# Work of GpSimd given to the vector engine, and identity products put between the tensor engine's products, in a four-layer network written by a build-time planner

## The chip, the cores and the metric

One core of a Trainium2 chip runs the whole network in one launch. The metric is the device time of that launch in microseconds (us), the median of several runs. The kernel before has a median of 1254.95 us in three runs (1254.81 to 1259.41).

## The reference

The input is a sequence of 256 rows of 1024 numbers, all fp32. It goes through two blocks of two layers each.

```python
def first_block(x, ...):
    for i in range(2):
        mix = even_mixer(rms_norm(x, norm_mix[i]), ...) if i == 0 else odd_mixer(...)
        x = x + mix
        x = x + sqrelu_mlp(rms_norm(x, norm_mlp[i]), mlp_w1[i], mlp_w2[i])
    return rms_norm(x, norm_final)

def second_block(x, ...):
    for layer in range(2):
        cols = split_columns(rms_norm_2(x, norm_g[layer]) @ w_in[layer])
        y_gdn, y_mla, y_rwkv = gdn_branch(cols, ...), mla_branch(cols, ...), rwkv7_branch(cols, ...)
        mix = concatenate([y_gdn, y_mla, y_rwkv], -1) * silu(cols['gate'])
        x = x + mix @ w_out[layer]
    return rms_norm_2(x, final_norm_g)
```

The even layer holds two kinds of attention with projected q, k, v (one of them over compressed keys too), the odd layer plain causal attention. The gated delta branch (gdn) and the rwkv branch are linear recurrences, evaluated in four chunks of 64 steps: inside a chunk a triangular system is inverted, and a state is carried from chunk to chunk, forward and backward in time. The mla branch is a softmax attention with rotary embeddings.

## The kernel before

The code names tiles and operations in program order. It does not say in which order an engine runs them. `Order.note` (line 265) records every operation with a cost that `Order.cost` (line 282) works out from its sizes, and `Order.plan` (line 396) then places them one by one: for each engine it takes, among the first operations whose inputs are ready, the one that can start earliest, and gives each new tile a place in SBUF or a bank in PSUM. It keeps its own clock for each engine, doubles the cost of a product where its own account of recent tensor work is low, and lengthens a vector operation that overlaps a GpSimd operation by its own account. `flush` (line 373) tries 24 ways of packing the memory, keeps the plan that it believes shortest, and issues all operations through `put` (line 560), so that nearly every row of the profile has the line L561. Semaphores are added from the tiles that operations share. Each engine runs its operations strictly in the planned order.

Within a layer, `weave` (line 1002) steps through parts named in a string ORDER (for instance `gdn_inv*2 rwkv_proj`), which gives the order of recording and with it the priority.

Weights come by `wload` (line 639): a transfer of 512 KB issued by SyncE into the tile wt, a copy on ScalarE that rounds it to fp32r (the tile fr), and a subtraction on VectorE for the rest; a product of full precision is three fp32r products (`mm3`, line 658). Products in plain fp32 appear in the trace with two records each. The q projection of the even layer (`Even.q`, line 1132) loads each half of its 256 columns in four transfers of 128 KB, with runs of 64 columns (256 bytes), in the order that its heads need.

The steps that the change and the prediction touch are these:

- `gdn_uw` (line 1843): the tiles kd[d] = kn * fd, 128x768, on GpSimd (line 1867), next to kg[d] on the vector engine.
- `gdn_steps` (line 1896): the state of the chunk before is scaled by ge into Sn, 128x384, on GpSimd (line 1935), and for one chunk an addition to qs (line 1945).
- `rwkv_prep` (line 2057): half of AR, a product of rT and ec, four times 128x256, on GpSimd (line 2111).
- `rwkv_bonus` (line 2186): an addition of 128x512 (line 2194), and for each half a scale and a product of 128x256 on GpSimd (lines 2198 and 2199). The bonus products of TensorE wait for them.
- `mla_proj` (line 2346): t1 + t2 of the rotary part, 128x256 and 64x256, on GpSimd (line 2444).
- `invert` (line 1586): the triangular inverse by substitution, 30 steps of one product and one addition each on the vector engine, every one needing the step before.
- `comp` (line 1326): 16 small products of 64x128 by 64x16, first the eight of the first half of the partitions, then the eight of the other.

What GpSimd does besides (the masks of `gdn_prep`, the gates of `rwkv_end` and `gdn_end`, some memsets, powers and weight transfers) is not touched.

Of the kernel before, what the change touches and what calls it, by code (L numbers as in the profile page):

```python
# [21 lines left out]
F = mybir.dt.float32  # L22
# [155 lines left out]
class Order:  # L178
# [4 lines left out]
    def __init__(self, nc, sb, wt, fr, ps):  # L183
# [17 lines left out]
        self.phase = 0.0  # L201
        self.ahead = 4000
# [62 lines left out]
    def note(self, eng, method, a, k):  # L265
# [4 lines left out]
        for key, v in k.items():  # L270
            if isinstance(v, bass.AP):
# [8 lines left out]
                         eng == "vector" and sum(self.space(x) == "sb" for x in ins if self.size(x) > 1) > 1))  # L280

    def cost(self, eng, method, outs, ins, k, ps):
# [90 lines left out]
    def flush(self):  # L373
# [16 lines left out]
        for i in self.log:  # L390
            eng, method, a, k = self.ops[i][:4]
            self.put(i, getattr(getattr(self.real, eng), method), [self.place(x) for x in a],
                     {q: self.place(x) for q, x in k.items()})
        self.ops = []

    def plan(self, preds, long, window=600, look=10):
# [35 lines left out]
        held = [0.0, 0.0]  # L432
# [10 lines left out]
        free, last_free = [0.0] * 16, 0.0  # L443

# [21 lines left out]
        while p < n:  # L466
            best = None
            for e in self.ENGINES:
                c, seen = None, 0
                for pr, i in avail[e]:  # L470
                    if i > p + window or seen >= look:
                        break
# [27 lines left out]
            avail[e].remove((pr, i))  # L500
            order.append(i)
# [11 lines left out]
            if method == "dma_start":  # L513
                dma = max(dma, s + cost + 650) + lat
                fin = dma + 900
            elif e == "tensor":
# [9 lines left out]
                gate[win] = gate.get(win, 0) + ops[i][10]  # L526
                fin = s + lat
            else:
                if e == "gpsimd":
                    held = [s, s + cost]  # L530
                elif e == "vector" and ops[i][12]:
                    slow = 0.5 * max(0.0, min(s + cost, held[1]) - max(s, held[0]))
                    cost, lat = cost + slow, lat + slow
                    if slow and now["gpsimd"] == held[1]:
                        held[1] += slow
                        now["gpsimd"] = held[1]
# [27 lines left out]
class Net:  # L564
# [74 lines left out]
    def wload(self, src, r0, nk, c0, nc_, pieces=None):  # L639
# [3 lines left out]
        for h in range(m):  # L643
# [8 lines left out]
            self.nc.scalar.copy(x[:, 0:n], raw)  # L652
            self.sub(x[:, n:2 * n], raw, x[:, 0:n].bitcast(F))
# [92 lines left out]
    def setup(self):  # L746
# [3 lines left out]
        nc.sync.dma_start(self.ident, I["consts"][:, 0:128])  # L750
        self.x = self.t(2048).rearrange("p (t d) -> p t d", t=2)
# [236 lines left out]
class Layer:  # L988

    tag = ""  # L990

    def __init__(self, net):
# [9 lines left out]
    def weave(self, order):  # L1002

        parts, ended = {}, set()
        for word in order.split():
            n, _, steps = word.partition("*")
            if n not in parts:
                m = n.rstrip("0123456789")
# [61 lines left out]
class Even(Layer):  # L1070

    tag = "E"
    ORDER = (
# [252 lines left out]
    def comp(self):  # L1326
# [4 lines left out]
        for g in range(2):  # L1331
            p = self.ps()
            sv = p[:, 0:128].rearrange("p (t j c) -> p t j c", t=2, j=4)
            sl = slice(g * 64, g * 64 + 64)
            for t in range(2):
                for j in range(4):
                    self.mm(sv[:, t, j, :], qT[sl, j, t * 128:(t + 1) * 128], self.ck[sl, :])
# [31 lines left out]
class Odd(Layer):  # L1369

    tag = "O"
    ORDER = (
# [63 lines left out]
class Second(Layer):  # L1436
# [4 lines left out]
    tag = "S"  # L1441

# [400 lines left out]
    def gdn_uw(self):  # L1843
# [52 lines left out]
    def gdn_steps(self):  # L1896
# [7 lines left out]
        for s in range(4):  # L1904
# [20 lines left out]
            if s < 3:  # L1925
# [8 lines left out]
                if s:  # L1934
                    self.mul(Sn, St, self.ge[:, s, :, :, None].to_broadcast([128, 2, 3, 64]), nc.gpsimd)
# [4 lines left out]
            if s:  # L1940
# [3 lines left out]
                if s == 2:  # L1944
                    self.add(qs[:, 1], qs[:, 1], dst, nc.gpsimd)
# [111 lines left out]
    def rwkv_prep(self):  # L2057
# [40 lines left out]
        for d in range(2):  # L2098
# [87 lines left out]
    def rwkv_bonus(self):  # L2186
# [7 lines left out]
        self.add(bo, av[0], av[1], nc.gpsimd)  # L2194
# [347 lines left out]
```

## Time and profile before

| what | value |
|---|---|
| median of three runs | 1254.95 us |
| the profiled execution | 1256.8 us |
| its span, first to last instruction | 1255.0 us |
| outside the span | 1.8 us |
| mean granted clock of TensorE | 0.902 of full speed |
| busy: TensorE, VectorE, ScalarE, GpSimd | 1073.0, 838.6, 576.5, 114.3 us |

In the profile PE is TensorE (PEld its weight loads), DVE is VectorE, ACT is ScalarE, POOL is GpSimd, SP is SyncE. The page's second part cuts the span in 40 slices of 31.4 us, one digit each. The granted clock has two levels, 1.2 and 2.4 GHz; 0.5 and 1.0 in a row are these two, and a number between them a stretch with both. The chain is the sequence of work that ended last, followed backward from the last instruction. A row of tensor work counts records, and busy time of the tensor engine is modelled, so that it may be stalled inside a busy stretch.

### The profile page before, as it was taken

What the parts mean: (1) busy time and instruction counts of PE and PEld (TensorE: products, weight loads), DVE (VectorE), ACT (ScalarE), POOL (GpSimd) and SP (SyncE); (2) the same over time, 40 slices, a digit from 0 to 9 for tenths busy, and PEclk for the clock granted to TensorE, in tenths of its full rate; (3) what the DMA queues carried; (4) which work ended last, traced back from release to release, by engine and by line L of the source; (5) the groups of instructions that cost most, each with busy time, mean ns of one, the idle gap of its engine ahead of it and who ended that gap; (6) DMA issues with size and microseconds to landing.
All of it is one profiled execution on the core that took longest, in us unless ns stands there. A gap on an engine that the chain in (4) does not pass through costs nothing.

```text
span 1255.0 us, 22363 instructions
## 1 busy us (share of the span) xinstructions
PE 1073.0 (85%) x8969; PEld 951.1 (76%) x8969; DVE 838.6 (67%) x1721; ACT 576.5 (46%) x1065; POOL 114.3 (9%) x182
## 2 busy tenths in 40 slices
PE   8998899999998999999997843488998894648895
PEld 7887699999897989999977743478668884647564
DVE  5556765555646585555579897863888899676646
ACT  4565454444427465444454532224574464222742
POOL 0000000000000000000013111002300312311100
PEclk9999899999998999999997965688999896777788
DMA  9930466555635335755743211122223342004100
GB/s 232 286 114 19 137 198 201 183 182 179 196 102 168 125 109 195 243 190 177 247 121 101 78 27 29 56 51 95 85 69 95 105 131 51 19 7 140 51 1 34
DMA packets 133905, 151.51 MB, mean 121 GB/s; under 512 B 24298, under 2 KB 115561, under 8 KB 133801
## 3 DMA queue, kind: packets, MB, share of 16 engines
q1 hardware_dynamic: 132969, 147.89, 37.9%
q0 software_dynamic: 832, 2.20, 0.6%
q8 instruction: 70, 1.15, 0.4%
q14 instruction: 34, 0.28, 0.1%
HBM read 147.42 MB, written 1.07 MB: 118 GB/s over the span
## 4 chain that ended last, share of the span: by engine, by line
PE 58%; DVE 25%; ACT 6%; issue 5%; DMA 4%; POOL 1%; SPq 1%; DVEq 0%; POOLq 0%; ACTq 0%
PE ps L561 58%; DVE sb L561 20%; DVE fr L561 5%; ACT sb L561 5%; DMA wt<-in_ev_w_in 2%; POOL sb L561 1%; ACT fr L561 1%; DMA wt<-in_mlp_w 1%; SPq L561 1%; DMA sb<-in_positions 1%; DMA wt<-in_w_in 0%; DMA sb<-in_norm_mlp 0%; ACT L561 0%; DMA brd<-sb 0%; DVEq L2538 0%
## 5 line engine op out<-in xcount | busy, mean ns | idle before, releaser
L561 PE MATMUL ps<-fr 128*128 128x256 f32 (+3 forms) x5112 | 791.5, 315 | 40.0 <-DVE sb L561 16.7
L561 PEld LDWEIGHTS ps<-fr 128*128 128x128 f32 (+1 forms) x5112 | 715.7, 194 | 100.2 <-DVE fr L561 17.2
L561 PE MATMUL ps<-sb 64*64 64x64 f32 (+12 forms) x3857 | 307.6, 285 | 131.1 <-DVE sb L561 97.2
L561 PEld LDWEIGHTS ps<-sb 64*64 64x64 f32 (+4 forms) x3857 | 240.5, 170 | 192.4 <-DVE sb L561 91.0
L561 DVE TENSOR_TENSOR fr<-wt,fr 128x1024 fp32r<-128x1024 f32 (+2 forms) x265 | 315.9, 1222 | 52.8 <-ACT fr L561 51.9
L561 ACT CAST fr<-wt 128x1024 fp32r<-128x1024 f32 (+2 forms) x265 | 262.5, 1034 | 71.0 <-DMA wt<-in_mlp_w 22.4
L561 ACT ACTIVATE sb<-sb 128x256 f32<-128x256 f32 (+7 forms) x347 | 163.3, 502 | 221.4 <-DVE sb L561 200.3
L561 DVE TENSOR_TENSOR sb<-ps,sb 128x256 f32<-128x256 f32 (+7 forms) x169 | 86.5, 518 | 170.9 <-ACT sb L561 91.7
L561 ACT ACTIVATE sb<-ps 128x384 f32<-128x384 f32 (+7 forms) x166 | 77.6, 475 | 247.3 <-PE ps L561 211.0
L561 DVE TENSOR_TENSOR sb<-sb 128x24 f32<-128x24 f32 (+27 forms) x408 | 142.4, 357 | 17.9 <-POOL sb L561 4.8
L561 DVE SCALAR_TENSOR_TENSOR sb<-sb 128x256 f32<-128x256 f32 (+8 forms) x228 | 94.8, 434 | 35.4 <-ACT sb L561 30.2
L561 POOL TENSOR_TENSOR sb<-sb 128x384 f32<-128x384 f32 (+4 forms) x83 | 88.0, 1080 | 294.8 <-DVE sb L561 184.1
L561 DVE TENSOR_TENSOR sb<-sb,ps 128x512 f32<-128x512 f32 (+3 forms) x82 | 46.8, 582 | 29.2 <-PE ps L561 28.9
L561 ACT ACTIVATE sb<-ps,sb 128x256 f32<-128x256 f32 (+3 forms) x70 | 35.0, 541 | 55.0 <-PE ps L561 48.2
L561 POOL TENSOR_SCALAR sb<-sb 128x2 f32<-128x2 f32 (+2 forms) x12 | 6.2, 515 | 415.3 <-DVE sb L561 304.4
L561 DVE TENSOR_TENSOR fr<-sb,fr 128x512 fp32r<-128x512 f32 (+1 forms) x38 | 24.7, 649 | 21.5 <-ACT fr L561 21.3
L561 POOL MEMSET sb<- 128x2 f32 (+3 forms) x59 | 5.6, 138 | 351.4 <-DVE sb L561 286.4
L561 ACT CAST fr<-sb 128x512 fp32r<-128x512 f32 x32 | 19.9, 622 | 31.5 <-DVE sb L561 31.5
L561 DVE COPY sb<-ps 128x384 f32<-128x384 f32 (+9 forms) x45 | 21.4, 478 | 17.0 <-PE ps L561 15.7
L561 DVE TENSOR_SCALAR sb<-sb 128x2 f32<-128x2 f32 (+15 forms) x115 | 27.2, 252 | 4.7 <-POOL sb L561 2.0
L561 DVE CUSTOM_DVE_ANT_0 sb<-ps,sb 128x128 f32<-128x128 f32 (+1 forms) x80 | 24.7, 353 | 6.7 <-PE ps L561 3.5
L561 ACT ACTIVATE fr<-ps,sb 128x256 fp32r<-128x256 f32 x52 | 19.8, 486 | 11.3 <-PE ps L561 10.6
(30 smaller groups left out, 162.7 us busy)
## 6 DMA issues: line engine op xcount, KB each, us to landing
wt<-in_mlp_w SPq DMA_DIRECT2D x128, 512.0 KB
wt<-in_w_in SPq DMA_DIRECT2D x38, 512.0 KB
wt<-in_od_w_in SPq DMA_DIRECT2D x24, 512.0 KB
wt<-in_w_out SPq DMA_DIRECT2D x16, 512.0 KB
wt<-in_ev_w_in SPq DMA_DIRECT2D x14, 512.0 KB
wt<-in_ev_w_out SPq DMA_DIRECT2D x8, 512.0 KB
wt<-in_od_w_out SPq DMA_DIRECT2D x8, 512.0 KB
wt<-in_w_in SPq DMA_DIRECT2D x8, 384.0 KB
```

The source lines that it names most:

```text
L561: fn(*a, **k)
```

## The change

There are six parts.

1. Five kinds of operation go from GpSimd to VectorE: kd in `gdn_uw`, Sn and the addition to qs in `gdn_steps`, half of AR in `rwkv_prep`, the addition, scales and products of `rwkv_bonus`, and t1 + t2 in `mla_proj`.

```diff
-            self.mul(f12(self.kd[d]), f12(kn), b(self.fd), self.nc.gpsimd)
+            self.mul(f12(self.kd[d]), f12(kn), b(self.fd))
...
-                    self.mul(Sn, St, self.ge[:, s, :, :, None].to_broadcast([128, 2, 3, 64]), nc.gpsimd)
+                    self.mul(Sn, St, self.ge[:, s, :, :, None].to_broadcast([128, 2, 3, 64]))
...
-                    self.add(qs[:, 1], qs[:, 1], dst, nc.gpsimd)
+                    self.add(qs[:, 1], qs[:, 1], dst)
...
-                self.mul(od(AR[h][:, :, 1, d], d), c4(rT[:, h]), ec[d][:, h, :, 1 - d:65 - d], nc.gpsimd)
+                self.mul(od(AR[h][:, :, 1, d], d), c4(rT[:, h]), ec[d][:, h, :, 1 - d:65 - d])
...
-        self.add(bo, av[0], av[1], nc.gpsimd)
+        self.add(bo, av[0], av[1])
...
-            self.ts(bo[:, h], bo[:, h], ka[:, h:h + 1], ka[:, 2 + h:3 + h], eng=nc.gpsimd)
-            self.mul(bo[:, h], bo[:, h], kT[:, h], nc.gpsimd)
+            self.ts(bo[:, h], bo[:, h], ka[:, h:h + 1], ka[:, 2 + h:3 + h])
+            self.mul(bo[:, h], bo[:, h], kT[:, h])
...
-            self.add(t1[:m], t1[:m], t2[:m], nc.gpsimd)
+            self.add(t1[:m], t1[:m], t2[:m])
```

2. The planner places products of the identity with itself. When it is about to place a tensor operation that it expects to start at s, it first fills the time up to s: as long as a product fits with 100 ns to spare, a PSUM bank is free, and its account of recent tensor work is under a limit, it issues one fp32 product of 128x128 by 128x128 into the bank that has been free longest. Nobody reads the result.

```diff
+            if e == "tensor" and hot and done[hot[0]] and uses[hot[1]]:
+                t, got = max(last_free, warm_from), self.arenas["ps"].find(1)
...
+                while got:
+                    t = max(t + self.switch(cut, (128, 128)), got[0])
...
+                    if t + took + self.spare > s or sum(x[1] for x in past) > self.dense * self.warm:
+                        break
+                    order.append(-1 - got[1][0])
...
+                    free, last_free, now[e] = [t] * 16, t, t
...
         for i in self.log:
+            if i < 0:
+                ar, x = self.arenas["ps"], self.place(self.idle)
+                self.real.tensor.matmul(ar.tile[:, (-1 - i) * ar.unit:(-1 - i) * ar.unit + 128], x, x, start=True, stop=True)
+                continue
```

3. The planner's costs change: a GpSimd operation is taken as shorter, and an overlap of the two engines lengthens both by factors that depend on the kind of vector operation.

```diff
-        c = 100 + n * per.get(method, 1.0) + (165 * n if k.get("op") == OP.pow else 0)
+        c = 60 + n * 0.8 * per.get(method, 1.0) + (165 * n if k.get("op") == OP.pow else 0)
...
+    def share(self, method, outs, ins):
+        if any(self.space(x) == "ps" for x in outs + ins):
+            return 0.0, 0.25
+        if method in ("tensor_copy", "tensor_scalar", "memset"):
+            return 0.75, 0.2
+        return (0.47, 0.5) if sum(self.size(x) > 1 for x in ins) > 1 else (0.0, 0.4)
```

4. The q weights of the even layer come in two transfers per half with runs of 128 columns (512 bytes). The reordering by heads moves into two copies and two subtractions of 128x512 with a stride in place of one each of 128x1024.

```diff
-        w = self.load(0, pieces=[(i * 64, (2 * c + i // 2 + 4 * (i % 2)) * 64, 64) for i in range(4)])
+        w = self.load(0, pieces=[(g * 128, (2 * c + 4 * g) * 64, 128) for g in range(2)], heads=True)
...
+                for j in range(2):
+                    self.nc.scalar.copy(xv[:, 0, :, j], rj[:, :, :, j])
+                    self.sub(xv[:, 1, :, j], rj[:, :, :, j], xv[:, 0, :, j].bitcast(F))
```

5. In `comp` the 16 small products alternate between the two halves of the partitions, into two banks.

```diff
+        for t in range(2):
+            for j in range(4):
+                for g in range(2):
+                    sl = slice(g * 64, g * 64 + 64)
+                    self.mm(svs[g][:, t, j, :], qT[sl, j, t * 128:(t + 1) * 128], self.ck[sl, :])
```

6. Assertions on the order of the parts are added, and a separate look-ahead for SyncE with the same value, 600, as the others had. The ORDER strings are the same.

## Rows read from the trace of the kernel before

**Rows 1.** The page's clock in 40 slices, chain by engine; span and clock by core.
```profile
PEclk9999899999998999999997965688999896777788
...
PE 58%; DVE 25%; ACT 6%; issue 5%; DMA 4%; POOL 1%; SPq 1%; DVEq 0%; POOLq 0%; ACTq 0%
...
core 0: 1255.0 us, clock 0.902
```

**Rows 2.** Busy time by stretch: length, PE, PEld, DVE, ACT, POOL, clock, DMA.
```profile
718.00:854.00 136.00, 76.04 (x1072) 68.91 (x1071) 102.41 (x229) 35.42 (x58) 11.75 (x12) 0.65 0.18 49
...
1038.00:1142.00 104.00, 57.62 (x986) 53.26 (x986) 76.63 (x172) 23.68 (x39) 26.81 (x26) 0.69 0.16 41
1158.00:1201.00 43.00, 36.96 (x294) 26.02 (x294) 23.38 (x66) 30.12 (x66) 6.61 (x9) 0.68 0.10 38
```

**Rows 3.** The chain's shares in the three stretches of rows 2, in order.
```profile
by line: DVE sb L561 46.4%; PE ps L561 33.3%; ACT sb L561 7.8%; issue 6.2%; DVE fr L561 4.7%; ACT fr L561 1.3%; DVEq L561 0.2%; ACTq L561 0.2%
...
by line: DVE sb L561 50.3%; PE ps L561 25.4%; POOL sb L561 9.6%; issue 7.6%; DVE fr L561 5.6%; ACT sb L561 2.2%; DVEq L561 0.1%; POOLq L561 0.1%
...
by line: PE ps L561 51.1%; DVE sb L561 27.8%; ACT sb L561 8.5%; issue 7.5%; DVE fr L561 5.8%; ACT fr L561 2.2%; DVEq L561 0.1%; ACTq L561 0.0%
```

**Rows 4.** Who TensorE waited for, whole span: total us, times, longest.
```profile
PE ps L561 <- DVE sb L561: 113.9, 52, 13.9
PE ps L561 <- ACT sb L561: 25.5, 26, 3.5
```

**Rows 5.** Columns of rows 2: two stretches of fp32r products, two of 64x64 products.
```profile
738.00:742.00 4.00, 4.00 (x21) 4.00 (x20) 3.91 (x11) 0.00 (x0) 0.00 (x0) 0.50 0.67 175
...
958.00:962.00 4.00, 4.00 (x36) 4.00 (x35) 4.00 (x11) 0.93 (x2) 0.00 (x0) 1.00 0.77 241
...
1090.00:1094.00 4.00, 4.00 (x108) 4.00 (x102) 1.18 (x2) 0.81 (x1) 0.00 (x0) 0.55 0.01 4
1094.00:1098.00 4.00, 2.60 (x99) 2.19 (x94) 2.57 (x3) 3.04 (x5) 0.52 (x1) 1.00 0.02 4
```

**Rows 6.** TensorE in order of time: start, length, form, records; the wait before.
```profile
946.35 1.93 PE L561 MATMUL ps<-sb 128*128 128x128 f32 x16
...
122.32 2.65 PE L561 MATMUL ps<-sb 64*128 64x16 f32 x24 [1.13 <-DVE sb L561]
```

**Rows 7.** GpSimd by form: busy us, mean ns of one, idle before.
```profile
L561 POOL TENSOR_TENSOR sb<-sb 128x256 f32<-128x256 f32 x26 | 25.7, 1004 | 143.8 <-DVE sb L561 71.5 <-ACT sb L561 59.2 <-PE ps L561 12.8
L561 POOL TENSOR_TENSOR sb<-sb 128x768 f32<-128x768 f32 x4 | 8.3, 2091 | 18.4 <-DVE sb L561 18.4
```

**Rows 8.** VectorE by form: busy us, mean ns of one, idle before.
```profile
L561 DVE TENSOR_TENSOR sb<-sb 128x256 f32<-128x256 f32 x34 | 15.2, 480 | 6.0 <-ACT sb L561 4.7 <-PE ps L561 1.0
...
L561 DVE TENSOR_SCALAR sb<-sb 128x256 f32<-128x256 f32 x22 | 7.6, 377 | 1.4 <-ACT sb L561 1.3
...
L561 DVE TENSOR_TENSOR sb<-sb 128x768 f32<-128x768 f32 x6 | 6.0, 1016 | 1.2 <-POOL sb L561 1.2
```

**Rows 9.** The chain near 1080 us, GpSimd's pieces, first and last: start, length.
```profile
1075.96 4.80 POOL sb L561 x2
...
1083.84 1.31 POOL sb L561
```

**Rows 10.** VectorE in order of time, with and without a 768-wide GpSimd operation beside.
```profile
728.51 1.42 DVE L561 TENSOR_TENSOR sb<-sb 128x58 f32<-128x58 f32 x1
...
730.18 0.20 DVE L561 TENSOR_TENSOR sb<-sb 128x58 f32<-128x58 f32 x1
```

**Rows 11.** DMA from 4 to 8 us, then from 48 to 52 us: packets, bytes, engines' share.
```profile
DMA packets 3132, 1.05 MB, mean 264 GB/s; under 512 B 2985, under 2 KB 3018, under 8 KB 3132
...
q1 hardware_dynamic: 3132, 1.05, 117.1%
...
DMA packets 1458, 1.46 MB, mean 364 GB/s; under 512 B 42, under 2 KB 1457, under 8 KB 1457
...
q1 hardware_dynamic: 1457, 1.45, 107.0%
```

More of the change, by code (lines that the diff above doesn't have):

```diff
@@ L201, in __init__ @@
         self.phase = 0.0
+        self.idle = None
+        self.dense, self.spare = 2.2, 100
+        self.reach = 600
         self.ahead = 4000
@@ L279, in note @@
                          self.mode(outs, ins) if eng == "tensor" else None,
-                         eng == "vector" and sum(self.space(x) == "sb" for x in ins if self.size(x) > 1) > 1))
+                         self.share(method, outs, ins) if eng == "vector" else None))
     def cost(self, eng, method, outs, ins, k, ps):
@@ L443, in plan @@
         free, last_free = [0.0] * 16, 0.0
+        hot, warm_from, past = None, 0.0, []
+        if self.idle is not None:
+            t = self.split(self.idle)[0]
+            hot = first[t], t
         def start(i, e):
@@ L469, in plan @@
                 c, seen = None, 0
+                far = p + (self.reach if e == "sync" else window)
                 for pr, i in avail[e]:
-                    if i > p + window or seen >= look:
+                    if i > far or seen >= look:
                         break
@@ L500, in plan @@
             avail[e].remove((pr, i))
+            if e == "tensor" and hot and done[hot[0]] and uses[hot[1]]:
+                t, got = max(last_free, warm_from), self.arenas["ps"].find(1)
+                past = [x for x in past if x[0] > t - 3413]
+                while got:
+                    t = max(t + self.switch(cut, (128, 128)), got[0])
+                    win = int((t + self.phase) / 3413.3)
+                    took = 420 if gate.get(win - 1, 0) < self.warm else 223
+                    if t + took + self.spare > s or sum(x[1] for x in past) > self.dense * self.warm:
+                        break
+                    order.append(-1 - got[1][0])
+                    cut = (128, 128)
+                    gate[win] = gate.get(win, 0) + 512
+                    past.append((t, 512))
+                    t += took
+                    free, last_free, now[e] = [t] * 16, t, t
+                    self.arenas["ps"].since[got[1][0]] = t + 200
+                    self.arenas["ps"].cache = {}
+                if cut is not None and ops[i][11][0] != cut:
+                    s = max(s, last_free + self.switch(cut, ops[i][11][0]))
             order.append(i)
@@ L515, in plan @@
                 fin = dma + 900
+                if hot and i == hot[0]:
+                    warm_from = fin
             elif e == "tensor":
@@ L529, in plan @@
                 if e == "gpsimd":
[L530 to L536, printed above, removed]
+                    more = sum(f * max(0.0, min(s + cost, y) - max(s, x)) for x, y, f in recent)
+                    cost, lat = cost + more, lat + more
+                    held = [s, s + cost, i]
+                elif e == "vector":
+                    f, g = ops[i][12]
+                    both = max(0.0, min(s + cost, held[1]) - max(s, held[0]))
+                    if both:
+                        cost, lat = cost + f * both, lat + f * both
+                        if now["gpsimd"] == held[1]:
+                            held[1] += g * both
+                            now["gpsimd"] = held[1]
+                            for j in succ[held[2]]:
+                                ready[j] = max(ready[j], held[1] + 50)
+                    recent.append((s, s + cost, g))
+                    del recent[:-8]
                 fin = s + lat
@@ L750, in setup @@
         nc.sync.dma_start(self.ident, I["consts"][:, 0:128])
+        self.order.idle = self.ident
         self.x = self.t(2048).rearrange("p (t d) -> p t d", t=2)
@@ L990 @@
     tag = ""
+    NEEDS = {}
     def __init__(self, net):
@@ L1007, in weave @@
             if n not in parts:
+                assert ended >= set(self.NEEDS.get(n, "").split()), (n, ended)
                 m = n.rstrip("0123456789")
@@ L1330, in comp @@
         nc.vector.memset(lc, BIG)
[L1331 to L1337, printed above, removed]
+        svs = [self.ps()[:, 0:128].rearrange("p (t j c) -> p t j c", t=2, j=4) for _ in range(2)]
+        for t in range(2):
[3 more added lines that the diff above has]
+                    self.mm(svs[g][:, t, j, :], qT[sl, j, t * 128:(t + 1) * 128], self.ck[sl, :])
+        for g, sv in enumerate(svs):
             hs = slice(g * 4, g * 4 + 4)
@@ L1371 @@
     tag = "O"
+    NEEDS = {"attn0": "proj0", "attn1": "proj1", "attn2": "proj2", "attn3": "proj3", "out_a": "attn0 attn1 attn2",
+             "out_b": "attn3"}
     ORDER = (
```

20 lines of the change are left out of this document (16 added, 4 removed).

## The prediction

> **What bounds the kernel now.** First the page: the chain that ends last is tensor work for 58% and vector work for 25%, and GpSimd is 1% of it [rows 1]. So this is a kernel bound by TensorE, with stretches in which VectorE sets the pace. The line of the granted clock shows where these lie: slices at 0.9 or full speed up to about 690 us, then slices of 0.5 to 0.8 in the two recurrent layers [rows 1]. A mean clock of 0.902 means that 2 x 0.098 x 1255 = 246 us were run at the lower level [rows 1]. Next the windows: three stretches, 718 to 854, 1038 to 1142 and 1158 to 1201 us, hold most of it: 136 x 0.70, 104 x 0.62 and 43 x 0.64 make 187 us at 1.2 GHz [rows 2]. In the first two VectorE is busy for 75%, and the tensor engine 56%. Last the chain in these stretches, since low clock costs nothing where TensorE is not on it: its share there is 33.3, 25.4 and 51.1% [rows 3].
>
> **The identity products.** They are placed where the planner expects TensorE to wait. It waits 139 us in 78 waits for VectorE and ScalarE [rows 4]. A product of this form is two records; 16 records of 128x128 took 1.93 us at full clock, so one takes 0.24 us [rows 6], and the waits hold at most 139 / 0.24 = 580. The clock was low in stretches where the engine did little before, so filling these waits should raise it.
>
> What a higher clock is worth: dense fp32r products ran at 21 records in 4 us at 0.50 and 36 at 1.00, 190 and 111 ns, so 42% is saved; packed 64x64 products at 37 ns at 0.55 and 26 ns at 1.00, 30% [rows 5]. Tensor work on the chain and at low clock is 136 x 0.333 x 0.70 + 104 x 0.254 x 0.62 + 43 x 0.511 x 0.64 = 31.7 + 16.4 + 14.1 = 62 us [rows 2, 3]. I scale this by 246/187 for the low clock outside the three stretches: 82 us. At 42% that is 34 us, the upper end; the lower end is 0, since nothing in this trace shows an identity product lifting the clock. With a mean of 36% it is 29 us, and I take half of that, **-14 us**, nearer to the middle than to either end: waits that are too short get no product, and where VectorE is busy three quarters of the time a quicker product soon meets it.
>
> Here the Trainium skill speaks for much more: in TensorE: Matmul & The Clock Gate, section Terms, the penalty of throttled time is given as that time times (1 - K/N). By it the 246 us would be worth 123 us. The rows do not bear this out, as most of that time is vector work on the chain; it stands as a rival below.
>
> What the products cost: each is in front of the next real product on TensorE's queue, and it waits for the last reader of its PSUM bank. The planner takes the bank that is free longest, so I cost that wait at nothing; if the reader is late, TensorE stands still behind it. A real product whose input lands while an identity product runs is late by half of one on average: 78 x 0.12 = 9 us if all these waits are on the chain [rows 4, 6]. Tensor work is about half of the chain, so **+4 us** (0 to 9, more if the plan is wrong, see the rivals).
>
> **Moved from GpSimd.** Per layer these are 2 products of 128x768, 3 operations of 128x384, 8 of 128x256 (one of these on 64 partitions), 1 of 128x512 and 2 scales of 128x256. On VectorE 768 takes 1.02, 256 takes 0.48 and the scale 0.38 us; between them I interpolate 0.61 for 384 and 0.75 for 512 [rows 8]. That makes 2.0 + 1.8 + 3.8 + 0.75 + 0.75 = 9.2 us per layer, 18.4 in both. Vector work is 46 to 50% of the chain there [rows 3], so about 9 us of this lands on it. What it gives back: GpSimd takes 2.09 us for 768 and 1.00 for 256 [rows 7], and from 1075.96 to 1085.15 its kd and bonus operations are the chain [rows 9], nearly all of the 9.6% of 104 us, 10 us, in rows 3. In VectorE's place the six of them on the chain (768 twice, scale and product of 256 twice) need 3.7 us, of which half is already counted: +2. Further, a vector addition of 58 columns took 1.42 us beside a 768-wide GpSimd operation and 0.20 after it [rows 10]; 1.2 us for each of four, of which half on the chain, gives -2.5. Sum 9 + 2 - 10 - 2.5 = **-2 us**; the ends are -12 (all additions hidden) and +8 (all 18.4 on the chain, no relief). What is left in GpSimd's queue, its weight transfers included, starts no later; it waits on VectorE or on tiles.
>
> Against this move stands a rule of the Trainium skill: Perfetto Trace Analysis, section Optimizing Scalar/DVE Operations, says that with a saturated DVE it can make sense to offload to Scalar or GPSIMD. VectorE is busy 75%, not saturated, in the stretches of rows 2; the same section warns that the two share a port, with which rows 10 agree. By the first half the sum of this part would be +8.
>
> **The q loads.** 16 transfers of 128 KB become 8 of 256 KB on SP's queue: half the issues, 8192 packets of 256 bytes become 4096 of 512. When the queue was full of short packets, 3132 of them took 117% of 16 engines for 4 us, 24 ns each; of about 1 KB, 1458 took 107%, 47 ns [rows 11]. A packet of 512 bytes then is some 31 ns, an estimate by a straight line: 8192 x 24 / 16 = 12.3 us become 4096 x 31 / 16 = 7.9. The start of the kernel waits for such loads, but partly for tensor work, so of 4.4 us saved I take **-2.5** (0 to -4.4). The additional copies and subtractions, twice 512 for 1024, cost a fixed part of some 0.1 to 0.2 us each, eight in all; loads and tensor work cover them, and uncovered they are 1.5 us.
>
> **The compressed scores.** 24 records took 2.65 us, one after the other [rows 6]; in pairs on two halves of the array half of it goes, at most -1.3, but the first addition then waits for more products: **-0.5**. The assertions and the look-ahead of the same value cost nothing, as no instruction comes of them. The changed planner costs issue nothing either, but any change of them reshuffles the order; I give that 0, with 7 us to either side, an estimate: half of the longest wait of TensorE, 13.9 us [rows 4].
>
> **Sum.** -14 + 4 - 2 - 2.5 - 0.5 = -15 against the profiled execution, 1256.8 us (span 1255.0 and 1.8 around it), 1241.8. The median stands 1.85 below that execution, so **1240 us**.
>
> **Rivals.** *The clock rises and all of it counts*: 29 to 34 us off, with the moves at their better end: 1214 to 1230. For it speaks that the third stretch has 51% of tensor work on its chain; against it, VectorE's 75%. Chance 0.15.
>
> *VectorE takes over*, or few products are placed: the 18.4 us all land on its chain, and what TensorE wins is waited for there; or the planner sees no pause or no bank. -14 becomes -5, the move +8, the rest -3 and tails +4: 1249 to 1261. For it speaks the vector share of 46 to 50% in rows 3. Chance 0.20.
>
> *Products stand in front of real work*: slower than before. The place is the recurrent layers. If the planner expects pauses longer than they are, the excess is paid in full: each hundredth of 139 us of waits is 1.4 us. The other terms give 19 us, so it decides from an excess of 14%, and at 25% the time is 1254.95 - 19 + 35 = 1271. For it: the plan runs open-loop over 1255 us, and if TensorE is later than planned, it does not wait where the plan has a pause. Against it: rows 10 show vector operations longer than the small time they take alone, which makes real pauses longer, not shorter. Chance 0.18, 1261 to 1285.
>
> *The full penalty*, all low clock worth half, 123 us: 1132. The chain rows speak against it. Chance 0.02.
>
> **How the numbers follow.** The forecast, 1230 to 1249, has 0.45. A measurement of this kernel can tell about 0.5%, 6.3 us, from no change: faster is below 1248.7, slower above 1261.2. Faster gets 0.45 + 0.15 + 0.02 = 0.62, same 0.20, slower 0.18. The range leaves out the far parts of the first and third rival and the fourth: 1217 to 1266; as most of the chance is on one side, the forecast's own range is 1230 to 1249.
>
> **What would show it.** Right: the mean clock over 0.95, the digits 5 to 7 in the slices from 690 us gone; 300 to 580 more products (twice as many records); GpSimd busy down by some 35 us to below 85; no GpSimd piece over 1 us in the chain near the bonus; fewer small packets. Wrong: a clock still near 0.90, or at 0.97 with the span unchanged (then vector work's share of the chain has risen), or waits of vector and scalar work on TensorE that have grown where identity products run. The forecast falls if the time is above 1249 or below 1230.

## The result, and the profile after

The changed kernel takes **1238.91 us**, median of four runs (1236.39 to 1240.92), against 1257.18 for the kernel before, run beside it. The ratio is 0.985, with a 95% interval of 0.9812 to 0.9887. A second measurement on another occasion gave 1237.09 us and 0.9836 (0.9811 to 0.986). The forecast was 1240.

The page of the changed kernel first, to be laid beside [rows 1]; operations are now issued from line 614, and the identity products are line 405, two records each.

```profile
PE 1095.4 (89%) x9257; PEld 974.2 (79%) x9257; DVE 835.9 (68%) x1757; ACT 576.5 (47%) x1069; POOL 74.9 (6%) x150
...
PEclk9999899999998999999999886889999788779798
...
DMA packets 129684, 151.54 MB, mean 123 GB/s; under 512 B 15979, under 2 KB 111338, under 8 KB 129578
...
L405 PE MATMUL ps<-sb 128*128 128x128 f32 x288 | 52.5, 336 | 16.7 <-DVE sb L614 13.9
```

Three things are to be seen. Only 144 products were placed (288 records), and the mean clock of this execution is 0.930, up from 0.902; digits of 6 to 8 remain from 690 us on. GpSimd lost 39 us of work, 114.3 before. And VectorE, which took over 32 operations, is busy for 835.9 us where it was 838.6 before: the work that came in does not show in its sum. The chain of waits of this trace breaks off at its first steps, so what follows goes by waits, windows and single instructions.

The waits of TensorE, as in [rows 4]: whom it waited for, total us, times, longest.

```profile
PE ps L614 <- DVE sb L614: 71.2, 34, 12.3
...
PE ps L405 <- DVE sb L614: 13.9, 5, 7.3
```

The first line was 113.9 us. The second is new: five times an identity product was itself kept waiting by VectorE, once for 7.3 us. The same stretches as in [rows 2], with the same columns (the work in them has moved up by 0 to 15 us):

```profile
718.00:854.00 136.00, 99.61 (x1409) 92.76 (x1409) 105.55 (x252) 38.97 (x64) 6.13 (x11) 0.82 0.23 59
1038.00:1142.00 104.00, 70.35 (x1217) 65.00 (x1215) 84.75 (x197) 26.38 (x44) 7.78 (x12) 0.82 0.16 45
1158.00:1201.00 43.00, 42.06 (x396) 29.42 (x392) 20.23 (x45) 28.47 (x77) 5.41 (x7) 0.92 0.19 63
```

The clock went from 0.65, 0.69 and 0.68 to 0.82, 0.82 and 0.92, while VectorE's share rose from 75 and 74% to 78 and 81% in the first two. TensorE in order of time, as in [rows 6], shows how a long pause is filled:

```profile
742.50 3.10 PE L405 MATMUL ps<-sb 128*128 128x128 f32 x16
750.07 2.04 PE L614 MATMUL ps<-sb 128*128 128x128 f32 x8 [4.47 <-DVE sb L614]
751.90 3.94 PE L405 MATMUL ps<-sb 128*128 128x128 f32 x20
761.80 2.00 PE L614 MATMUL ps<-sb 32*32 32x32 f32 x64 [5.95 <-DVE sb L614]
```

The products stand at the beginning of the pause, and 4.5 and 6.0 us stay empty behind them. The code says why: within one pause the account of recent tensor work only grows, and stops the filling. Of VectorE's forms of [rows 8], the two that most of the moved work has:

```profile
L614 DVE TENSOR_TENSOR sb<-sb 128x256 f32<-128x256 f32 x48 | 18.5, 419 | 3.8 <-ACT sb L614 3.6
L614 DVE TENSOR_TENSOR sb<-sb 128x768 f32<-128x768 f32 x10 | 9.2, 955 | 0.0
```

Each is more numerous and its mean shorter than before (480, 1016 ns).

### The profile page after: what moved, and what is told of

It is laid out like the page before. It is cut to its first block, busy times and chain, and to the rows that moved or that the text cites. A ratio compares the mean times of both kernels' runs of the same rounds, so it can differ in the third digit from the quotient of the medians.

```text
span 1234.6 us, 22911 instructions
## 1 busy us (share of the span) xinstructions
PE 1095.4 (89%) x9257; PEld 974.2 (79%) x9257; DVE 835.9 (68%) x1757; ACT 576.5 (47%) x1069; POOL 74.9 (6%) x150
## 2 busy tenths in 40 slices
DMA packets 129684, 151.54 MB, mean 123 GB/s; under 512 B 15979, under 2 KB 111338, under 8 KB 129578
## 5 line engine op out<-in xcount | busy, mean ns | idle before, releaser
L614 PE MATMUL ps<-sb 64*64 64x64 f32 (+13 forms) x3857 | 292.9, 273 | 86.1 <-DVE sb L614 56.0
L614 DVE TENSOR_TENSOR fr<-wt,fr 128x1024 fp32r<-128x1024 f32 (+4 forms) x269 | 315.5, 1205 | 67.8 <-ACT fr L614 67.4
L614 PEld LDWEIGHTS ps<-sb 64*64 64x64 f32 (+4 forms) x3857 | 226.5, 159 | 144.8 <-DVE sb L614 59.8
L614 ACT CAST fr<-wt 128x1024 fp32r<-128x1024 f32 (+4 forms) x269 | 262.9, 1022 | 79.9 <-DMA wt<-in_mlp_w 29.2
L614 ACT ACTIVATE sb<-sb 128x256 f32<-128x256 f32 (+8 forms) x347 | 163.3, 503 | 220.4 <-DVE sb L614 195.1
L614 DVE TENSOR_TENSOR sb<-sb 128x256 f32<-128x256 f32 (+27 forms) x436 | 148.9, 355 | 15.6 <-POOL sb L614 5.0
L405 PE MATMUL ps<-sb 128*128 128x128 f32 x288 | 52.5, 336 | 16.7 <-DVE sb L614 13.9
L614 POOL TENSOR_TENSOR sb<-sb 128x384 f32<-128x384 f32 (+4 forms) x55 | 53.4, 989 | 221.0 <-PE ps L614 130.1
L405 PEld LDWEIGHTS ps<-sb 128*128 128x128 f32 x288 | 46.5, 241 | 19.9 <-DVE sb L614 11.3
L614 DVE TENSOR_SCALAR sb<-sb 128x256 f32<-128x256 f32 (+16 forms) x119 | 26.6, 241 | 5.7 <-ACT sb L614 2.9
```

The source lines that it names most:

```text
L405: self.real.tensor.matmul(ar.tile[:, (-1 - i) * ar.unit:(-1 - i) * ar.unit + 128], x, x, start=True, stop=True)
L614: fn(*a, **k)
```

## The experiments

Two theories were set against each other from the start: that the gain is the products' (by the clock), or that it is the move's (VectorE no longer slowed). Runs that keep the order of the real work differ from their base only in the identity products or in the engine of the named operations; where the planner ran anew, that is said. The ratio behind each time is to the kernel before, run beside it (1255.3 to 1258.7 us); between runs of different occasions it is the ratio that should be compared.

**The products taken out.** The planner still places them, so the order is that of the changed kernel; they are not issued. Run twice, the second time beside the changed kernel on the same chip.

```diff
             if i < 0:
+                continue
                 ar, x = self.arenas["ps"], self.place(self.idle)
```

> The changed kernel with its planned order kept to the last operation, but the 144 identity products not issued. Theory (the products raise the clock and that is the largest part of the gain): the mean clock falls from 0.930 back to about 0.90 and the time rises by about 10 us against the changed kernel, to 1249 (14 us of clock lost, 4 us of delays behind products won back). Rival 1 (the gain is the new order and the moved operations, the products only colour the clock rows): the clock falls, but the time stays within 3 us of 1239. Rival 2 (the products mostly stand in front of real work): the time falls, to 1234 or less.

> The changed kernel once more, beside the two runs below on the same chip, as the base for them. Ratio to the kernel before as it was, 0.981 to 0.989.

> The changed kernel with its 144 identity products left out at issue, the order of real work unchanged, beside the changed kernel on one chip. If the products are worth the 5.5 us that the first comparison gave: 4 to 8 us above the changed kernel. If what stands in front of real work pays back all that the clock gives, as in the kernel before with filled pauses: within 2 us of it. If the forecast's net term was right: 10 us above.

Measured: 1244.44 us, 0.9898 (0.9871 to 0.9926); then 1244.21, 0.9907 (0.9873 to 0.9942), beside 1237.09 with the products. By the medians they are worth 5.5 us in the first comparison and 7.1 in the second (6.0 and 8.9 by the ratios). The intervals of the first pair overlap, those of the second just miss each other. For the second pair, the page's rows and then the waits of TensorE for VectorE, first without products, then with:

```profile
PE 1072.0 (86%) x8969; PEld 950.5 (77%) x8969; DVE 833.9 (67%) x1757; ACT 576.8 (46%) x1069; POOL 75.7 (6%) x150
```

```profile
PE ps L615 <- DVE sb L615: 101.2, 40, 11.8
```

```profile
PE 1096.1 (89%) x9257; PEld 974.2 (79%) x9257; DVE 836.8 (68%) x1757; ACT 576.3 (47%) x1069; POOL 74.0 (6%) x150
...
L405 PE MATMUL ps<-sb 128*128 128x128 f32 x288 | 50.9, 328 | 16.7 <-DVE sb L614 14.1
```

```profile
PE ps L614 <- DVE sb L614: 72.9, 37, 12.2
...
PE ps L405 <- DVE sb L614: 14.1, 5, 7.3
```

With products the real tensor work is busy for 1096.1 - 50.9 = 1045.2 us in place of 1072.0, 27 us less. The span is 1236.6 in place of 1241.0, only 4.4 us less, as the products take 50.9 us and the engine's idle time fell by 28.5 only (169.0 to 140.5). The low clock went from 2 x 0.099 x 1241 = 246 us to 2 x 0.067 x 1236.6 = 166 us. By the rule of the Trainium skill (TensorE: Matmul & The Clock Gate, section Terms) those 80 us are worth 40, an estimate. The runs give 5.5 to 7.1, net of what the products cost, so here it overstates several times over.

Where the gain arises can be read off, as the same real product can be found in both traces. Each time without products first, then with:

```profile
676.21 7.62 PE L615 MATMUL ps<-sb 128*128 128x6 f32 x30 [1.95 <-DVE sb L615]
...
722.75 0.89 PE L615 MATMUL ps<-sb 64*64 64x128 f32 x24
...
1205.14 0.68 PE L615 MATMUL ps<-sb 64*64 64x64 f32 x16
```

```profile
673.96 4.04 PE L614 MATMUL ps<-sb 128*128 128x6 f32 x30 [0.28 <-DVE sb L614]
...
719.68 0.89 PE L614 MATMUL ps<-sb 64*64 64x128 f32 x24
...
1202.07 0.68 PE L614 MATMUL ps<-sb 64*64 64x64 f32 x16
```

One batch of 30 records of 128x6, with 11 identity products in the two pauses before it, takes 4.04 us in place of 7.62, at a clock of 1.00 in place of 0.50; in the first comparison it is 4.86 in place of 7.62. At about 720 us the kernel with products is 3.1 us ahead (3.2 in the first comparison), and at the end of the forecast's third stretch still 3.1 (4.2). So from the start of the first to the end of the third of the stretches from which the forecast took most of its clock term, they gave 0 to 1 us. The rise of the clock in these stretches is not all theirs either: without products this order already has 0.72, 0.75 and 0.87 there, against 0.65, 0.69 and 0.68 in the order before.

**More products.** Three ways: the account of recent work pruned inside a pause, which makes the planner work anew (216 products); the changed kernel's own order with every pause filled to its end (382 products); each of the 144 products issued twice.

```diff
                 while got:
+                    past = [x for x in past if ...]
```

> The changed kernel with one line more in the planner: inside the loop that places products the account of recent tensor work forgets what is old, so that a long pause is filled to its end (216 products planned in place of 144). The order is planned anew. Theory: the clock rises from 0.93 to 0.95 or more and the time falls by 3 to 8 us, to about 1233. Rival 2 (delays eat it): 1239 to 1246 at the higher clock. Rival 1 (the clock is not what gives the time): the same time within 3 us at the higher clock.

```diff
+                if got:
+                    x = t
+                    while x + 260 + self.spare <= s:
+                        order.append(-1 - got[1][0])
+                        x += 260
```

> The order of real operations is that of the changed kernel; only the pauses are filled to their end, with 382 identity products in place of 144. Theory (the products gave 5.5 us rather than 10 net because a long pause is filled only for its first microseconds): the mean clock goes from 0.930 to 0.95 or more and the time falls 2 to 7 us below the changed kernel's 1238.9, to 1232 to 1237. Rival (what is in front of real work eats what the clock gives): the clock rises as well, but the time is 1239 to 1250, and TensorE's waits of VectorE shrink by more than the span does.

```diff
                 self.real.tensor.matmul(ar.tile[...], x, x, start=True, stop=True)
+                self.real.tensor.matmul(ar.tile[...], x, x, start=True, stop=True)
```

> The changed kernel with each of its 144 identity products issued twice, in the same places. If a product in front of real work costs what the forecast took (half a product late for each pause, and the end of the pause rarely overrun), the added 144 cost 0 to 5 us against the changed kernel's 1238.9, less what the clock gives: 1237 to 1243. If the plan's pauses are already overrun, each added product of 0.24 to 0.34 us is paid in full where TensorE is on the chain: 144 x 0.29 = 42 us busy, half of it on the chain, so 1255 to 1262.

Measured: 1245.75 us, 0.9899 (0.9873 to 0.9925), at a clock of 0.926; 1240.82, 0.9893 (0.9867 to 0.9918), at 0.949; 1240.25, 0.9873 (0.9845 to 0.99), at 0.936. None is faster than the changed kernel. In the first the order is another one as well, so it tells little. The second keeps the order, and its rival won: the clock rose and the time did not fall. One place shows most of it. It is the end of a substitution, where VectorE keeps TensorE waiting; TensorE in order of time, without products, in the changed kernel, and with filled pauses:

```profile
805.53 1.56 PE L615 MATMUL ps<-sb 64*64 64x64 f32 x48 [7.22 <-DVE sb L615]
...
817.93 0.63 PE L615 MATMUL ps<-fr 128*128 128x320 f32 x1
```

```profile
800.36 2.50 PE L405 MATMUL ps<-sb 128*128 128x128 f32 x10 [7.29 <-DVE sb L614]
802.79 1.56 PE L614 MATMUL ps<-sb 64*64 64x64 f32 x48
...
814.06 0.41 PE L614 MATMUL ps<-fr 128*128 128x320 f32 x1
```

```profile
805.18 9.96 PE L405 MATMUL ps<-sb 128*128 128x128 f32 x64 [7.29 <-DVE sb L619]
815.07 0.93 PE L619 MATMUL ps<-sb 64*64 64x64 f32 x48
...
824.27 0.41 PE L619 MATMUL ps<-fr 128*128 128x320 f32 x1
```

The products meant for this pause wait for the last reader of their bank, and that reader is VectorE at the end of the same substitution. So they start when the pause is over, in front of the batch of 48 records. From the end of the wait to the fp32r product it takes 12.40 us without products, 13.70 with, and 19.09 with filled pauses, although the batch itself then runs in 0.93 us in place of 1.56. That is a loss of 5.4 us between the second and the third, in one place. The trace of the third is that of its slowest execution (1246.07 us); it is 9.7 us longer than that of the changed kernel, of which 3 us are lost by 82 us (see the last section), and behind 854 us it gains 0.3 us on it. The run of doubled products lay within its first expectation.

**Products alone.** The kernel before, its order and its GpSimd work unchanged, with 362 products in its pauses, placed by a loop like the one above.

> The kernel before, with its order and its GpSimd work unchanged, and 362 identity products in its pauses. Theory (products are worth some 5 us by themselves, a few more when the pauses are filled to their end): clock from 0.902 to 0.95, time 5 to 10 us below the kernel before, 1249 to 1254 against 1258.7. If the forecast's term was right for a full set of products (14 less 4): 1245 to 1249. Rival (delays eat it, since this plan knows less of how the two engines slow each other): 1258 to 1268 with the clock up.

Measured: 1255.97 us, ratio 1.0004 (0.9982 to 1.0026).

```profile
PE 1151.6 (91%) x9693; PEld 1029.5 (82%) x9693; DVE 838.9 (67%) x1721; ACT 576.3 (46%) x1065; POOL 113.5 (9%) x182
...
L394 PE MATMUL ps<-sb 128*128 128x128 f32 x724 | 103.1, 301 | 15.7 <-DVE sb L580 13.0
```

The clock is 0.940, and real tensor work is busy for 1151.6 - 103.1 = 1048.5 us, 24.5 less than before; and nothing comes of it. Both gains that were expected of this run failed to come; the rival holds, by the ratio at its lower end. A clock that rises is no gain by itself. Two things can have taken it, and this run does not separate them: the quicker products waited for VectorE, or the added ones stood in front of others.

**The move alone.** First the kernel before, its order unchanged: the 32 operations are planned on GpSimd as they were, and issued to VectorE. Then the reverse in the changed kernel: the 32 go back to GpSimd at their places.

```diff
             eng, method, a, k = self.ops[i][:4]
+            eng = "vector" if i in self.swapped else eng
...
```

> The kernel before with its planned order kept, the 32 operations of part 1 issued to the vector engine at their old places in the order, nothing else changed. Theory: a gain of 2 us, 1255, with GpSimd busy about 75 instead of 114 us and the chain near 1080 us without its 9 us of GpSimd. Rival 1 (moves are the main gain): 1247 or less. Rival 3 (vector engine is the bound, all 18 us land on the chain): 1262 or more.

> The changed kernel with its planned order kept, but the 32 moved operations issued to GpSimd again. Theory: 2 to 5 us more than the changed kernel, 1241 to 1244, as the plan gives GpSimd no time of its own for them. Rival 1 (moves are the main gain): 1247 or more. Rival 3 (the vector engine pays for them): below 1236.

Measured: 1248.93 us, 0.9931 (0.9908 to 0.9953), 9.8 us below the 1258.7 beside it; and 1251.38, 0.9949 (0.9932 to 0.9966), which is 12.5 us above the changed kernel. So the move is the larger half of the gain, in either order. Of VectorE's forms, with busy us and mean ns, three in the kernel before, then with the move alone. None of the 32 has one of these forms, so the operations are the same in both.

```profile
L561 DVE TENSOR_TENSOR sb<-ps,sb 128x256 f32<-128x256 f32 x66 | 27.6, 420 | 32.0 <-PE ps L561 31.7
...
L561 DVE TENSOR_TENSOR sb<-sb 128x220 f32<-128x220 f32 x16 | 7.4, 460 | 0.2
...
L561 DVE TENSOR_TENSOR sb<-sb 128x58 f32<-128x58 f32 x16 | 4.7, 292 | 0.3
```

```profile
L567 DVE TENSOR_TENSOR sb<-ps,sb 128x256 f32<-128x256 f32 x66 | 27.5, 419 | 31.8 <-PE ps L567 31.3
...
L567 DVE TENSOR_TENSOR sb<-sb 128x220 f32<-128x220 f32 x16 | 6.1, 383 | 0.2
...
L567 DVE TENSOR_TENSOR sb<-sb 128x58 f32<-128x58 f32 x16 | 3.4, 214 | 0.3
```

The two forms with both inputs in SBUF became 17 and 27% shorter; the form with one input in PSUM did not change. The Trainium skill states this (SBUF — State Buffer, section Who interferes with whom): a vector instruction with two SBUF inputs contends with a GpSimd instruction that reads SBUF, one with at most one SBUF input, outside certain modes, does not. The trace agrees for these three forms. Not every form follows so plainly: 128x384 with two SBUF inputs stayed at 552 and 551 ns, and a copy of 128x512 with one fell from 675 to 418; whether it ran in one of those modes no row shows. The account, with the page's row of the move alone:

```profile
PE 1073.1 (86%) x8969; PEld 952.5 (76%) x8969; DVE 837.6 (67%) x1753; ACT 576.4 (46%) x1065; POOL 76.2 (6%) x150
```

The 32 operations cost VectorE 16.6 us by the means of their forms in this run (four of 768 at 951 ns, six of 384 at 551, fourteen of 256 at 420, two of 512 at 687, four scales at 347, two on 64 partitions at 414), and its busy time fell by 1.0. So by this estimate 17.6 us of slowing went with 38.1 us of GpSimd work, **0.46 us for each us**. Given back in the changed kernel, the same operations have this row:

```profile
PE 1104.5 (88%) x9257; PEld 982.5 (79%) x9257; DVE 835.9 (67%) x1725; ACT 577.0 (46%) x1069; POOL 103.8 (8%) x182
```

VectorE is rid of 32 operations, 17.2 us by the means of the changed kernel, and is busy as long as with them; GpSimd has 28.9 us more. That is 0.59 for each.

The chain of waits from 1060 to 1100 us shows the other half, [rows 9]: GpSimd is not on it any more, and the batch of TensorE that waited for it starts 4.3 us earlier. One batch near 1038 us, and this one in the chain, in the kernel before, then with the move alone:

```profile
1038.46 7.27 PE L561 MATMUL ps<-fr 128*128 128x256 f32 x46 [0.63 <-DVE fr L561]
...
1086.91 7.08 PE ps L561 x171
```

```profile
1038.00 7.27 PE L567 MATMUL ps<-fr 128*128 128x256 f32 x46 [0.63 <-DVE fr L567]
...
1078.58 3.94 DVE sb L567 x8
...
1082.57 3.00 PE ps L567 x68
```

Up to 1038 us the two traces are within 0.5 us of each other, although the first of the two recurrent layers lies before it: there the moved work and the relief of VectorE cancel. At 1060 us the lead is 1.2 us, behind this place 4.3, and at the end 8.1. Of the rest 2.8 us come near 1190 us, where TensorE's clock was 0.60 before and 1.00 with the move; whether that belongs to the move or to the execution, one trace of each does not tell.

**The rest of GpSimd's work moved too.** The changed kernel, its order unchanged, with another 46 operations issued to VectorE: the masks of `gdn_prep` and the gates of `gdn_end` and `rwkv_end`, in the same manner.

> The changed kernel with the elementwise operations that GpSimd still has in the recurrent layers (masks, two gates; some 45 operations of 256 to 512 columns, 47 us of GpSimd) issued on the vector engine at their places in the order. Theory (what the move gave was vector operations no longer slowed, a third of the GpSimd time that goes, and GpSimd's slower pieces out of the chain): about 45 x 0.5 = 22 us of vector work come in, 14 to 16 us of slowing go, and these masks stand less on the chain than kd and the bonus did, so the time stays within 4 us of the changed kernel or falls by up to 4. Rival (VectorE is the bound there, 22.4 of 24 us busy from 666 to 690): 8 to 20 us above it.

Measured: **1233.32 us**, 0.9796 (0.9773 to 0.9819), 3.8 us below the changed kernel on the same chip; the two intervals overlap, so that the step is a gain is likely rather than certain; the loss of 8 us or more that the rival had is excluded. It is the fastest version of all runs. Its trace is that of the slowest of its six executions (1239.84 us), so the gain does not show in the trace's span, and the account goes by busy time:

```profile
PE 1103.2 (89%) x9257; PEld 980.4 (79%) x9257; DVE 838.2 (68%) x1803; ACT 576.5 (47%) x1069; POOL 29.1 (2%) x104
```

The 46 operations are 23.9 us by their forms (32 of 384 at 549 ns, twelve of 256 at 415, two of 512 at 684). VectorE's busy time rose by 2.3 us above 835.9. So 21.6 us of slowing went with 74.9 - 29.1 = 45.8 us of GpSimd work, 0.47 for each (0.50 against the second trace of the changed kernel, with 836.8 and 74.0): near the price of the first set, and more relief than the 14 to 16 us that the theory had. The stretch that the rival named, in the changed kernel and then here, columns of [rows 2]:

```profile
655.00:700.00 45.00, 38.95 (x271) 36.13 (x271) 42.28 (x108) 21.75 (x44) 11.75 (x19) 0.89 0.37 106
```

```profile
655.00:700.00 45.00, 39.88 (x274) 36.80 (x273) 41.98 (x122) 21.80 (x44) 1.56 (x11) 0.89 0.36 106
```

VectorE does 14 operations more, and is busy no longer.

**The planner's costs alone.** The kernel before with part 3 of the change, planned anew; nothing moved, no products.

```diff
-        c = 100 + n * per.get(method, 1.0) + (165 * n if k.get("op") == OP.pow else 0)
+        c = 60 + n * 0.8 * per.get(method, 1.0) + (165 * n if k.get("op") == OP.pow else 0)
...
```

> The kernel before with the changed costs of the planner alone (GpSimd's shorter, overlaps lengthening both engines by kind of operation), planned anew; nothing is moved, no products, loads as before. Theory (a new order is worth up to some 7 us to either side, as the forecast had it): 1252 to 1266 against 1258.7. Rival (the better account of the two engines is itself a large part of the gain): 1245 to 1251.

Measured: 1256.78 us, 1.0007 (0.9989 to 1.0025). No gain by itself.

**Surer banks.** The version with the masks moved; no products in a bank that the plan has free for less than 2.9 us, the other pauses filled to their end.

```diff
+                late = got and t - got[0] < 2900
...
-                    order.append(-1 - got[1][0])
+                    order.append(-1 - got[1][0] - 8 * late)
...
             for i in self.log:
+                if i < -8:
+                    continue
```

> The changed kernel with the masks and gates on the vector engine as in the run before, the same order of real work, and another choice of identity products: none where the plan has the bank free for less than 2.9 us before the pause (75 of the 144 go, among them the ten at 800 and 805 us and the others whose start waits for VectorE), and the pauses with a surer bank are filled to their end: 198 products in all. Theory (the full filling lost its gain in one place, where 32 products waited 7.3 us for the reader of their bank and then ran for 9.96 us in front of real work): mean clock at or above the 0.926 of the run before, no wait of an identity product for VectorE above 1 us, and 1 to 5 us below that run's ratio of 0.9796, so 0.9756 to 0.979. Rival (TensorE's quicker products are met by VectorE wherever they stand): 0.979 to 0.982, with the clock up. Second rival (the products that go were worth having, as the clock stays low through the substitution): above 0.982.

Measured: 1234.96 us, 0.9807 (0.978 to 0.9834), clock 0.925. No identity product waits for VectorE now, but the theory did not hold: the ratio is not below 0.9796, and the clock did not rise. Two things were changed at once, the products taken away and those added elsewhere. From 795 to 815 us, with all products and then with the sure ones:

```profile
795.00:815.00 20.00, 10.63 (x189) 9.24 (x189) 14.61 (x35) 0.00 (x0) 0.00 (x0) 0.83 0.16 41
```

```profile
795.00:815.00 20.00, 9.24 (x190) 8.33 (x190) 16.41 (x41) 0.39 (x1) 0.00 (x0) 0.50 0.15 37
```

Without the late products the clock stays at its lower level to the end of the substitution. In these two traces what they cost in front of the batch and what they gave behind it come out even: the run with the sure ones is 2.1 us behind the other both at 764 and at 841 us.

## Why the prediction was right, and where its steps were not

The time was right, as a sum of terms of which the largest were far off in opposite directions; that they cancelled to within 3 us is luck.

**The identity products, -14 and +4.** Measured together: -5.5 to -7.1. The sign was right, and the speeds of [rows 5] were reached, with the 64x64 batch at 0.93 us in place of 1.56. Mis-sized was the share of the clock's worth that reaches the end: I took half of 29 us. The products made real tensor work 27 us shorter, and a fifth to a quarter of that arrived. The place was wrong too: about half of the lead or more arises at 640 to 720 us, and over the three stretches that I had counted, where VectorE holds a quarter to a half of the chain [rows 3], 0 to 1 us. I also expected 300 to 580 products and a clock over 0.95; 144 were placed, as the account stops them. That this limit was no loss is shown by the filled pauses: 382 products, 0.949, no faster. The step "the planner takes the bank that is free longest, so I cost that wait at nothing" failed: five times the bank's reader was late, 13.9 us in all. That is not all loss, as the real product behind can have to wait as well: at 805 us it waited 7.22 us without products.

**The moves, -2.** Measured: -9.8 in the order of before, -12.5 in the new one, at and beyond the end of -12 that I had drawn. (The four numbers of this term add up to -1.5, taken as -2.) What came in was sized well (18.4 us forecast, 16.6 found). Mis-sized was the relief: I priced it at four additions of 58 columns [rows 10], -2.5 us, where 17.6 us of VectorE's time went, as much as came in. So of the +9 for moved work on the chain nothing is to be seen up to 1038 us. I had read one pair of rows as an incident. The -10 for GpSimd's pieces was put on one place near 1080 us, less +2 for VectorE in their stead; in the traces 3.1 us of the lead arise there. The rule that spoke against the move (the Trainium skill, Perfetto Trace Analysis, section Optimizing Scalar/DVE Operations) would have made this term +8; the runs decide against offloading here, and for that section's own warning about the shared port.

**The q loads and `comp`, -3.** The small packets went as said: 15979 below 512 bytes, 24298 before. No run has these two parts alone, but the traces show what became of them. Both lie in the first of the four layers. The product of TensorE that follows `comp`, in the kernel before, then in the second run without products:

```profile
129.65 0.69 PE L561 MATMUL ps<-sb 128*128 128x128 f32 x2 [4.68 <-DVE sb L561]
```

```profile
129.95 0.69 PE L615 MATMUL ps<-sb 128*128 128x128 f32 x2 [7.39 <-DVE sb L615]
```

TensorE came there earlier, and waited longer for VectorE; what the loads and `comp` had won was gone. In the first run without products it stands at 129.21, in the move alone at 129.90. So of the term of -3 these traces show nothing that is left.

**The order, 0 with 7 to either side.** The costs alone cost 0.0007 of the time, within the interval of nothing. The runs that have everything but the products (1244.2 to 1244.4) stand 0.0024 to 0.0033 in ratio below the one with the move alone (0.9931), 3 to 4 us; the intervals overlap. As the three traces are still within 1.3 us of each other at 646 us, before the recurrent layers, that difference would be that of the new order of the work in these layers; no run has this alone.

**The rivals.** "Products stand in front of real work" was right in part, and wrong in size for 144 products; with 382 it ate the gain (ratio 0.9893, against 0.9898 and 0.9907 without any). The reason seen was not a pause shorter than planned but the late reader of a bank. "VectorE takes over" was right for the products and wrong for the move, which relieved VectorE. The full penalty is excluded by the runs.

**The signs.** GpSimd below 85 us: right, 74.9. The clock over 0.95 and the low digits gone: wrong, and the time was right in spite of it, so the clock was a poor sign to choose.

The parts are so: the move 9.8, the products 5.5 to 7.1, the new order with loads and `comp` 3 to 4, together 18 to 21 us, against 18 and 20 in the two measurements of the whole. As each part is the step from one run to the next, that they add up is no test of them.

## What to carry to other kernels

Before giving elementwise work to GpSimd, compare the means of VectorE's two-input forms in stretches with and without it: here each microsecond of GpSimd took 0.46 to 0.59 from VectorE, and about half as much time on VectorE did the same work, so the offload saved nothing there even with VectorE the bound. Products that only keep the clock up are worth what the chain of tensor work is worth behind them, not what the clock shows; many of them in a bank whose last reader is the engine that causes the pause are a loss (32 cost 5.4 us more there than five). To see where a change gains, follow the same instruction through both traces when the order is kept. A right total can hide two wrong terms: only single parts, in the same order of instructions, show it.

## What was not expected of the hardware

Replacing GpSimd's operations one for one left VectorE's busy time within 2.3 us of where it was, three times, at 0.46, 0.47 and 0.59 us of slowing for each us of GpSimd; I had not expected the work that came in and the slowing that went to be so nearly equal.

The clock also differs between traces in a place that the change hardly touches. From 74 to 82 us the changed kernel and the one with filled pauses ran the same order, with no identity product in that stretch:

```profile
74.00:82.00 8.00, 8.00 (x70) 7.81 (x67) 0.95 (x2) 3.06 (x7) 0.00 (x0) 1.00 0.01 2
```

```profile
74.00:82.00 8.00, 8.00 (x47) 7.20 (x47) 0.95 (x2) 1.46 (x7) 0.00 (x0) 0.62 0.00 0
```

TensorE was busy throughout both and got through 70 records at full clock, 47 at 0.62. The kernel before and its version with products differ in the same way there. Of the fourteen traces four have it, at 0.60 to 0.83: the three with pauses filled to their end, and the one in which the 32 operations went back to GpSimd, with the changed kernel's 144 products. Whether it is chance or follows from what TensorE did earlier is not shown. It moves what comes after by 2 to 3 us, and is one reason why differences of 2 us stay unsettled above.
